# Where the feed-forward's operands begin in on-chip memory: one small tile made 96 bytes longer

## The chip, the cores and the metric

The kernel runs on one core of a Trainium2 chip. TensorE (PE in the profile) multiplies, VectorE (DVE) and ScalarE (ACT) work on elements, SyncE (SP) issues most of the transfers, GpSimd (POOL) a few. A matrix product takes two instructions: one loads the stationary operand of 128 x 128 into the array (PEld in the profile), one streams the moving operand of up to 512 columns past it (PE). Both operands are read from the on-chip memory, in which every tile takes the same bytes on each of 128 partitions; "the place" of a tile is the byte at which it begins on a partition.

The metric is the device time of one execution in microseconds (us); a lower time is better.

## The reference, cut to what matters

One layer of a hybrid backbone for 1024 latent tokens and 256 context tokens of width 1024. Two token mixers (a gated linear attention and a gated delta rule) read the normalised input, their outputs are merged and projected by `w_out`, and a SwiGLU feed-forward and a final norm follow. The part that this change bears on:

```python
x = x + mod_l[2] * y_l                       # y_l = merged @ w_out
x = x + mod_l[5] * swiglu(modulate(rmsnorm(x, norm2_w), mod_l[3], mod_l[4]),
                          ffn_w_gate, ffn_w_up, ffn_w_down)
return rmsnorm(x, final_norm_w)

def swiglu(t, w_gate, w_up, w_down):
    return (jax.nn.silu(t @ w_gate) * (t @ w_up)) @ w_down
```

`x` is 1024 x 1024, `w_gate` and `w_up` are 1024 x 2816, `w_down` is 2816 x 1024, all float32.

## The kernel before, in words

There are three phases, one after the other. Phase 1 normalises the input, projects it and runs the gated linear attention; phase 2 runs the gated delta rule and the gates; phase 3, from about 1575 us on, is the output projection, the second norm and the feed-forward.

A float32 product is made of three products in a rounded format (`mm3`, lines 167 to 173): each operand is split into a high part (rounded by ACT) and a low part (what is left, by DVE), and high x high (L171), high x low (L172) and low x high (L173) add up in one bank of PSUM. So the large products are long rows of one form of matmul: 128 x 128 stationary, 512 columns moving, each with a weight load of its own. In the names of the profile, `ch<-hh,whi` is a matmul into a bank `ch`, with `hh` moving and `whi` stationary. Trailing numbers are left out, so `hh` stands for `hh0` and `hh1`.

In phase 3:

- **Output projection** (L1134 to L1136): stationary is the merged mixer output in `hh`/`hl` (high and low), moving is `w_out`, which lies in `xh`/`xl`. 8 token tiles x 2 halves x 24 matmuls, 384 in all, in banks `pj`.
- **Second norm** (`norm2`, L1145): after each two token tiles, DVE works out the norm's factors, PE turns the tokens with a diagonal matrix (L1161, plain float32), and ACT and DVE write the high and low part back into `hh`/`hl`, which from then on hold the normalised input.
- **Gate and up projection** (L1184 to L1192): for each of 22 tiles of the hidden width, 16 stationary blocks of each weight (`whi`, `wlo`, split from `wraw` at L153 and L154 into a ring of four buffers), the normalised input `hh`/`hl` moving, in two halves of 512 tokens. 22 x 2 x 2 x 24 = 2112 matmuls, in banks `ch` (gate) and `pj` (up).
- **Down projection** (L1207 to L1213): the activations (kept in `xh`) are stationary, the rows of `w_down` (kept in `xl`) move. The 22 tiles come in groups of 2 or 3, and after each group DVE adds the 16 partial results to `x1`. In the last group the final norm and the store of each token tile follow at once.

Where things lie is decided by pools, which stack in the order in which they are opened; a tile takes its bytes rounded up to 32. In phase 3 the order is `xp` (`xh`, `xl`), `x1p`, `wp2` (the weights' `wraw`, `whi`, `wlo`), `f1` (`a2`, `m5`, `fw`, `ms3`, `mh`, `rs3`), `hp` (`hh0`, `hh1`, `hl0`, `hl1`), `f2` (the rest). All tiles of `xp`, `x1p` and `wp2` have lengths that are multiples of 2048 bytes; so have those in front of the weights in phases 1 and 2. `f1` takes 32 + 4096 + 4096 + 32 + 64 + 32 = 8352 bytes, which is 65 x 128 + 32. From the built program, in bytes:

| tiles | begin at | remainder by 128 | remainder by 512 |
|---|---|---|---|
| `xh`, `xl` (all phases) | 18112, 50880 | 64 | 192 |
| `whi`, `wlo` of phase 1, first buffers | 104128, 112320 | 64 | 192 |
| `whi`, `wlo` of phase 3, first buffers | 120512, 128704 | 64 | 192 |
| `hh0`, `hh1`, `hl0`, `hl1` | 145248 + i x 16384 | 96 | 352 |
| `draw`, `a`, `tmp2`, `junk3` in `f2` | from 210784 | 96 | 352 |

The blocks that one matmul or one weight load takes out of these tiles begin at multiples of 512 bytes from the tile's start, so the remainders hold for each of them.

Of the kernel before, what the change touches and what calls it, by code (L numbers as in the profile page):

```python
# [8 lines left out]
F32 = mybir.dt.float32  # L9
# [8 lines left out]
P = 128  # L18
# [57 lines left out]
class Layer:  # L76
# [1095 lines left out]
    def ffn(self, f1, f2, x1, hh, hl):  # L1172
        nc, I = self.nc, self.I
        m5 = f1.tile([P, D], F32, name="m5")
        nc.sync.dma_start(m5, self.mrow[5].broadcast_to([P, D]))
        fw = f1.tile([P, D], F32, name="fw")
        nc.sync.dma_start(fw, I['final_norm_w'].rearrange("(o n) -> o n", o=1).broadcast_to([P, D]))
        groups = [range(a, b) for a, b in zip((0, 2, 4, 7, 10, 13, 16, 19), (2, 4, 7, 10, 13, 16, 19, 22))]
        ms = f1.tile([P, 8], F32, name="ms3")
        mh = f1.tile([P, 8, 2], F32, name="mh")  # L1180
        rs = f1.tile([P, 8], F32, name="rs3")
        for gi, g in enumerate(groups):
            acts, downs = [], []
            for f in g:  # L1184
                wg = self.wcols(I['ffn_w_gate'], f * P)
                wu = self.wcols(I['ffn_w_up'], f * P)
                ah, al = self.xh[:, f % 4, :], self.xh[:, 4 + f % 4, :]
                for n in range(2):
                    ns = slice(n * 512, n * 512 + 512)
                    pg, pu = self.ch(P, 512), self.pj(P, 512)  # L1190
                    for ps, w in ((pg, wg), (pu, wu)):
                        self.mm3(ps, [(w[k][0], w[k][1], hh[n][:, k, :], hl[n][:, k, :]) for k in range(KT)])  # L1192
                    a = f2.tile([P, 512], F32, tag="a", name="a", bufs=4)
                    nc.scalar.activation(a, pg, AF.Tanh, scale=0.5)
                    nc.vector.scalar_tensor_tensor(a, a, 1.0, pg, ALU.add, ALU.mult)
                    nc.vector.tensor_tensor(a, a, pu, ALU.mult)  # L1196
                    nc.scalar.activation(ah[:, ns], a, AF.Copy)  # L1197
                    nc.vector.tensor_tensor(al[:, ns], a, ah[:, ns].bitcast(F32), ALU.subtract)
                acts.append((ah, al))
                raw = f2.tile([P, D], F32, tag="draw", name="draw")  # L1200
                nc.sync.dma_start(raw, I['ffn_w_down'][f * P:(f + 1) * P, :])
                nc.vector.tensor_tensor(raw, raw, m5, ALU.mult)
                dh, dl = self.xl[:, f % 4, :], self.xl[:, 4 + f % 4, :]
                nc.scalar.activation(dh, raw, AF.Copy)  # L1204
                nc.vector.tensor_tensor(dl, raw, dh.bitcast(F32), ALU.subtract)
                downs.append((dh, dl))
            for t in range(8):  # L1207
                ts = slice(t * P, t * P + P)
                for n in range(2):
                    ns = slice(n * 512, n * 512 + 512)  # L1210
                    ps = (self.pj if gi == len(groups) - 1 and n else self.wk)(P, 512)
                    self.mm3(ps, [(a[0][:, ts], a[1][:, ts], w[0][:, ns], w[1][:, ns]) for a, w in zip(acts, downs)])
                    nc.vector.tensor_tensor(x1[:, t, ns], x1[:, t, ns], ps, ALU.add)  # L1213
                    if gi == len(groups) - 1:
                        junk = f2.tile([P, 512], F32, tag="a", name="junk3", bufs=4)
                        nc.scalar.activation(junk, x1[:, t, ns], AF.Square, accum_out=mh[:, t, n:n + 1])
                if gi == len(groups) - 1:
                    m, r = ms[:, t:t + 1], rs[:, t:t + 1]
                    nc.vector.tensor_tensor(m, mh[:, t, 0:1], mh[:, t, 1:2], ALU.add)
                    nc.vector.tensor_scalar(m, m, 1.0 / D, EPS, ALU.mult, ALU.add)  # L1220
                    self.rsqrt(f2, r, m, 1, "fr")
                    nc.vector.scalar_tensor_tensor(x1[:, t, :], x1[:, t, :], r, fw, ALU.mult, ALU.mult)  # L1222
                    nc.sync.dma_start(self.out[ts, :], x1[:, t, :])
# [35 lines left out]
```

## Time and profile before

| | |
|---|---|
| median of 3 runs | 2439.49 us (2432.53 to 2444.21) |
| profiled execution | 2438.06 us, of which its span is 2436.3 us |
| PE busy in the span | 2346.7 us (96%) |
| DVE, ACT busy | 65%, 45% |
| mean granted TensorE clock | 0.987 of full speed |

How to read it: the share of busy time of PE hides how fast it works, since consecutive matmuls overlap in the records (a record of 0.39 us is followed by the next one 0.23 us later). What a stretch of matmuls costs is read from the starts of its first and last matmul and their number. An engine's row ends with the idle time before its instructions and with what released them; idle time of an engine that PE does not wait for costs nothing.

### The profile page before, as it was taken

The page shows a single profiled execution, that of the slowest core. Times are in us where ns is not written, and L with a number is a line of the kernel's source. Part 1 is how long each engine was busy: PE and PEld are TensorE (multiplying, and loading weights), DVE is VectorE, ACT ScalarE, POOL GpSimd, SP SyncE. Part 2 cuts the span into 40 slices and gives each one's busy share as a digit, 9 for nine tenths or more (in the row PEclk, how much of TensorE's full clock was granted, in tenths as well). Part 3 has the DMA queues.
Part 4 walks back from the last instruction along what each step waited for, and adds up shares of the span by engine and source line. Part 5 has one row for each costly group of instructions (what it writes and reads, how often), then busy time and mean ns, then how long its engine had stood idle before and what let it go on. Part 6 is the DMA issues. An engine that isn't in the chain of part 4 may idle for free. (4 is left out here: it accounts for less than half of the span.)

```text
span 2436.3 us, 37019 instructions
## 1 busy us (share of the span) xinstructions
PE 2346.7 (96%) x13868; PEld 1932.4 (79%) x13868; DVE 1583.7 (65%) x3855; ACT 1100.0 (45%) x2691; POOL 68.7 (3%) x138
## 2 busy tenths in 40 slices
PE   7999999999999889999999999899999999999998
PEld 5978988988988668777777877677888888888886
DVE  6479589489499577888888876655543434334336
ACT  7265165265265556876886676433112112121112
POOL 0000000000000000000000000000000000000000
PEclk9999999999999999999999999899999999999999
DMA  8212412313312532333333233241211111111101
GB/s 286 67 29 71 141 27 89 120 27 102 115 27 90 168 104 76 112 88 103 92 94 115 76 93 100 78 147 36 60 36 55 52 39 57 40 56 48 35 27 69
DMA packets 199106, 197.77 MB, mean 81 GB/s; under 512 B 13715, under 2 KB 166619, under 8 KB 198927
## 3 DMA queue, kind: packets, MB, share of 16 engines
q1 hardware_dynamic: 186096, 159.12, 21.9%
q0 software_dynamic: 10016, 35.19, 4.1%
q8 instruction: 109, 1.79, 0.3%
q10 hardware_dynamic: 2815, 1.11, 0.2%
q14 instruction: 70, 0.57, 0.1%
HBM read 164.13 MB, written 31.23 MB: 80 GB/s over the span
## 5 line engine op out<-in xcount | busy, mean ns | idle before, releaser
L171 PE MATMUL pj<-xh,whi 128*128 128x512 f32 x1040 | 426.1, 410 | 4.9 <-ACT cout L785 3.2
L173 PE MATMUL pj<-xh,wlo 128*128 128x512 f32 x1040 | 424.0, 409 | 2.8 <-DVE wlo L154 2.8
L172 PE MATMUL pj<-xl,whi 128*128 128x512 f32 x1040 | 424.7, 408 | 0.2 <-DVE xl L333 0.2
L153 ACT ACTIVATE whi<-wraw 128x512 fp32r<-128x512 f32 x232 | 145.8, 630 | 304.7 <-PE pj L172 109.9
L154 DVE TENSOR_TENSOR wlo<-wraw,whi 128x512 fp32r<-128x512 f32 x232 | 159.0, 690 | 120.3 <-ACT whi L153 119.4
L171 PEld LDWEIGHTS pj<-xh,whi 128*128 128x128 f32 x1040 | 198.0, 190 | 38.1 <-ACT cout L785 3.8
L173 PEld LDWEIGHTS pj<-xh,wlo 128*128 128x128 f32 x1040 | 197.4, 190 | 35.6 <-DVE wlo L154 3.1
L172 PEld LDWEIGHTS pj<-xl,whi 128*128 128x128 f32 x1040 | 197.9, 190 | 31.9 <-DVE xl L333 0.5
L1213 DVE TENSOR_TENSOR x<-x,wk 128x512 f32<-128x512 f32 x120 | 82.5, 687 | 113.7 <-PE wk L173 113.4
L171 PE MATMUL ch<-hh,whi 128*128 128x512 f32 x352 | 139.6, 397 | 0.0
L172 PE MATMUL ch<-hl,whi 128*128 128x512 f32 x352 | 139.6, 397 | 0.0
L171 PE MATMUL pj<-hh,whi 128*128 128x512 f32 x352 | 139.6, 397 | 0.0
L172 PE MATMUL pj<-hl,whi 128*128 128x512 f32 x352 | 139.6, 397 | 0.0
L173 PE MATMUL pj<-hh,wlo 128*128 128x512 f32 x352 | 139.6, 397 | 0.0
L173 PE MATMUL ch<-hh,wlo 128*128 128x512 f32 x352 | 139.6, 396 | 0.0
L171 PE MATMUL wk<-xl,xh 128*128 128x512 f32 x328 | 127.7, 389 | 0.0
L172 PE MATMUL wk<-xl,xh 128*128 128x512 f32 x328 | 127.7, 389 | 0.0
L173 PE MATMUL wk<-xl,xh 128*128 128x512 f32 x328 | 127.6, 389 | 0.0
L793 DVE SCALAR_TENSOR_TENSOR cout<-cin,cw,cout 128x896 f32<-128x896 f32 (+1 forms) x96 | 113.4, 1181 | 3.7 <-ACT cout L785 3.7
L1204 ACT ACTIVATE xl<-draw 128x1024 fp32r<-128x1024 f32 x22 | 22.5, 1054 | 196.6 <-PE wk L173 189.2
L1196 DVE TENSOR_TENSOR a<-a,pj 128x512 f32<-128x512 f32 x44 | 30.3, 688 | 114.4 <-PE pj L173 114.4
L1197 ACT ACTIVATE xh<-a 128x512 fp32r<-128x512 f32 x44 | 27.8, 632 | 128.4 <-DVE a L1196 128.4
(392 smaller groups left out, 5458.9 us busy)
## 6 DMA issues: line engine op xcount, KB each, us to landing
wraw<-in_w_in_dram SPq DMA_DIRECT2D x144, 256.0 KB, 3.0
mw<-in_w_mod_dram SPq DMA_DIRECT2D x64, 256.0 KB, 4.0
wraw<-in_ffn_w_gate_dram SPq DMA_DIRECT2D x44, 256.0 KB, 2.9
draw<-in_ffn_w_down_dram SPq DMA_DIRECT2D x22, 512.0 KB, 4.0
wraw<-in_ffn_w_up_dram SPq DMA_DIRECT2D x44, 256.0 KB, 2.9
bc<-rows SPq DMA_DIRECT2D x80, 128.0 KB, 3.1
wm<-in_w_mod_dram SPq DMA_DIRECT2D x16, 512.0 KB, 3.7
A<-rows SPq DMA_DIRECT2D x64, 128.0 KB, 3.2
```

Source lines behind the costliest of these rows:

```text
L153: nc.scalar.activation(hi, raw, AF.Copy)
L154: nc.vector.tensor_tensor(lo, raw, hi.bitcast(F32), ALU.subtract)
L171: self.nc.tensor.matmul(ps, ah, bh, start=(first and i == 0), stop=False)
L172: self.nc.tensor.matmul(ps, ah, bl, start=False, stop=False)
L173: self.nc.tensor.matmul(ps, al, bh, start=False, stop=(last and i == n - 1))
L793: nc.vector.scalar_tensor_tensor(o, cl[:, :, lo + s:16 + hi + s], tap(i), o, ALU.mult, ALU.add)
L1196: nc.vector.tensor_tensor(a, a, pu, ALU.mult)
L1197: nc.scalar.activation(ah[:, ns], a, AF.Copy)
L1204: nc.scalar.activation(dh, raw, AF.Copy)
L1213: nc.vector.tensor_tensor(x1[:, t, ns], x1[:, t, ns], ps, ALU.add)
```

## The change

The tile `ms3`, which holds one number per token tile for the final norm, gets 32 columns of float32 where it had 8. The code still uses columns 0 to 7. The same instructions stand in the same order on every engine, with the same shapes.

```diff
         groups = [range(a, b) for a, b in zip((0, 2, 4, 7, 10, 13, 16, 19), (2, 4, 7, 10, 13, 16, 19, 22))]
-        ms = f1.tile([P, 8], F32, name="ms3")
+
+        ms = f1.tile([P, 32], F32, name="ms3")
         mh = f1.tile([P, 8, 2], F32, name="mh")
         rs = f1.tile([P, 8], F32, name="rs3")
```

`f1` then takes 8448 bytes = 66 x 128, and what is allocated behind `ms3` moves up by 96 bytes: `mh` and `rs3`, then `hh` and `hl`, then all of `f2`. `hh0` begins at 145344, with a remainder of 64 by 128 and of 448 by 512; the tiles `draw`, `a`, `tmp2` and `junk3` of `f2` get the remainder 64 by 128 too. `xh`, `xl`, `x1` and the weights stay where they are.

## Rows read from the trace of the kernel before

**Rows 1.** The page: the span, PE's busy time, and the granted clock in 40 slices of the span.

```profile
span 2436.3 us, 37019 instructions
...
PE 2346.7 (96%) x13868; PEld 1932.4 (79%) x13868; DVE 1583.7 (65%) x3855; ACT 1100.0 (45%) x2691; POOL 68.7 (3%) x138
...
PEclk9999999999999999999999999899999999999999
```

**Rows 2.** The view of waits for PE alone, from 1686 us to the end: all that it lists (us in total, times, longest).

```profile
PE wk L1161 <- issue: 1.0, 1, 1.0
```

**Rows 3.** The page's groups by line: two of the six groups of the gate and up projection (each x352) and one of the three of the down projection; busy us, mean ns of one record, idle before.

```profile
L171 PE MATMUL ch<-hh,whi 128*128 128x512 f32 x352 | 139.6, 397 | 0.0
...
L173 PE MATMUL pj<-hh,wlo 128*128 128x512 f32 x352 | 139.6, 397 | 0.0
...
L171 PE MATMUL wk<-xl,xh 128*128 128x512 f32 x328 | 127.7, 389 | 0.0
```

**Rows 4.** The timeline of PE from 1935 to 1975 us, inside the gate and up projection of one group of tiles: start us, length us, line, operands. First two and last of 172 consecutive matmuls.

```profile
1934.78 0.40 PE L172 MATMUL pj<-hl,whi 128*128 128x512 f32 x1
1935.01 0.40 PE L173 MATMUL pj<-hh,wlo 128*128 128x512 f32 x1
...
1974.84 0.40 PE L172 MATMUL pj<-hl,whi 128*128 128x512 f32 x1
```

**Rows 5.** The same view from 1897 to 1912 us, inside a down projection: first and last of 68 consecutive matmuls.

```profile
1896.81 0.39 PE L171 MATMUL wk<-xl,xh 128*128 128x512 f32 x1
...
1911.99 0.39 PE L172 MATMUL wk<-xl,xh 128*128 128x512 f32 x1
```

**Rows 6.** The same view from 1643 to 1664 us, inside the output projection: three of a stretch that repeats itself, and the ends of 90 consecutive matmuls.

```profile
1642.83 0.40 PE L171 MATMUL pj<-xh,hh 128*128 128x512 f32 x1
...
1645.41 0.39 PE L173 MATMUL pj<-xh,hl 128*128 128x512 f32 x1
1645.64 0.40 PE L171 MATMUL pj<-xh,hh 128*128 128x512 f32 x1
1645.88 0.39 PE L172 MATMUL pj<-xl,hh 128*128 128x512 f32 x1
...
1663.61 0.40 PE L173 MATMUL pj<-xh,hl 128*128 128x512 f32 x1
```

**Rows 7.** The same view in phase 1, 740.5 to 744 us: a projection that follows other matmuls. Between the first and the second row shown lie 8 matmuls, between the second and the third 3.

```profile
740.86 0.40 PE L173 MATMUL pj<-xh,wlo 128*128 128x512 f32 x1
...
742.94 0.39 PE L173 MATMUL pj<-xh,wlo 128*128 128x512 f32 x1
...
743.85 0.39 PE L171 MATMUL pj<-xh,whi 128*128 128x512 f32 x1
```

**Rows 8.** Busy time in three stretches of 10 us: two in down projections and one in a gate and up projection. Columns: stretch, its us, then busy us and (instructions) of PE, PEld, DVE, ACT, POOL, then granted clock, DMA share, GB/s.

```profile
1802.00:1812.00 10.00, 10.00 (x46) 8.28 (x45) 6.18 (x10) 1.26 (x2) 0.00 (x0) 1.00 0.17 49
1900.00:1910.00 10.00, 10.00 (x46) 8.29 (x45) 3.24 (x6) 0.00 (x0) 0.00 (x0) 1.00 0.01 2
1760.00:1770.00 10.00, 10.00 (x44) 8.05 (x43) 4.07 (x6) 1.23 (x2) 0.00 (x0) 1.00 0.35 105
```

**Rows 9.** Groups by line: the output projection's first products over the whole run, and all its matmuls from 1578 to 1592 us.

```profile
L171 PE MATMUL pj<-xh,hh 128*128 128x512 f32 x128 | 52.9, 415 | 4.3 <-ACT hh L1122 3.4 <-DVE d L1138 0.9
...
L171 PE MATMUL pj<-xh,hh 128*128 128x512 f32 x15 | 7.4, 502 | 3.4 <-ACT hh L1122 3.4
L172 PE MATMUL pj<-xl,hh 128*128 128x512 f32 x14 | 6.3, 464 | 0.0
L173 PE MATMUL pj<-xh,hl 128*128 128x512 f32 x13 | 5.9, 457 | 0.0
```

**Rows 10.** The timeline around the last second norm: PE's turn of the tokens.

```profile
1695.82 2.02 PE L1161 MATMUL wk<-diag,x 128*128 128x128 f32 x16 [0.98 <-issue]
```

**Rows 11.** The view of waits from 1735 to 2395 us: what the weights' split and the rows of `w_down` waited for.

```profile
ACT whi L153 <- PE pj L172: 75.8, 39, 2.2
...
DVE draw L1202 <- DMA draw<-in_ffn_w_down_dram: 14.6, 11, 2.6
```

**Rows 12.** Groups by line of ACT and DVE with the same work on tiles of either remainder: `wraw`, `whi`, `wlo` have 64, `a` has 96.

```profile
L154 DVE TENSOR_TENSOR wlo<-wraw,whi 128x512 fp32r<-128x512 f32 x232 | 159.0, 690 | 120.3 <-ACT whi L153 119.4
...
L1198 DVE TENSOR_TENSOR xh<-a,xh 128x512 fp32r<-128x512 f32 x44 | 30.4, 692 | 17.2 <-ACT xh L1197 15.4
L1197 ACT ACTIVATE xh<-a 128x512 fp32r<-128x512 f32 x44 | 27.8, 632 | 128.4 <-DVE a L1196 128.4
```

**Rows 13.** The end: PE's last matmul in the timeline, and the last step of the chain that ended last.

```profile
2424.41 0.39 PE L173 MATMUL pj<-xl,xh 128*128 128x512 f32 x1
...
2431.21 1.28 DVE x L1222
```

## The prediction

> **What bounds the kernel now.** I read the page first: PE is busy for 2346.7 of 2436.3 us, at the full clock in nearly every slice [rows 1]. Then the waits for PE in phase 3: from 1686 us to the end it waits once, for 1.0 us [rows 2]. So the feed-forward takes as long as its matmuls take, and no transfer, split or bank holds it up. What remains is how fast one matmul follows another. The groups by line hint at a difference: the same form of matmul has records of 397 ns in the gate and up projection and of 389 ns in the down projection [rows 3]. Records overlap, so I took the timeline and divided the time between two starts by the number of steps:
>
> - gate and up, 171 steps: (1974.84 - 1934.78) / 171 = 234.3 ns [rows 4];
> - down, 67 steps: (1911.99 - 1896.81) / 67 = 226.6 ns [rows 5];
> - output projection, 89 steps: (1663.61 - 1642.83) / 89 = 233.5 ns [rows 6].
>
> The form, the clock and the number of weight loads are the same in all three. The neighbours' work doesn't sort them: the down stretch at 1802 us has 6.18 us of DVE and 1.26 us of ACT in 10 us, the one at 1900 us has 3.24 and nothing, and both start 46 matmuls; the gate and up stretch at 1760 us, with DVE between the two (4.07), has 44 [rows 8]. The bank doesn't either: phase 1 projects into `pj`, as the output projection does, and gets to the fast step there: after other work, 9 steps in (742.94 - 740.86) us or 231 ns each, then 4 in (743.85 - 742.94) us or 227.5 ns, which is 226.6 within the rounding of the rows [rows 7].
>
> What does sort them is where the two operands lie. Down (`xl` moving, `xh` stationary) and phase 1 (`xh` and the weights) have both operands at remainder 64 by 128 bytes: 226.6 ns. Gate and up (`hh` 96, weights 64) and the output projection (`xh` 64, `hh` 96) have them 32 bytes apart: 234.3 and 233.5 ns. The output projection is the telling one, since there `hh` is stationary and the other operand moves. My reading: while one matmul streams, the next one's weights are read from the same memory; with equal remainders the two reads fall into a step that hinders them least after a few matmuls, with unequal ones they never do.
>
> **The change part by part.**
>
> *Gate and up.* `hh` and `hl` get the weights' remainder, so I let these matmuls go at the down projection's step: 6 groups of 352 are 2112 matmuls [rows 3], 2112 x (234.3 - 226.6) ns = 16.3 us. Nothing of it lies beside other work, since PE waits for nothing there. The two ends: if each of them stayed in what phase 1 shows ahead of the fast step, 231 ns [rows 7], it would be 2112 x 3.3 = 7.0 us; by the records' means, 397 against 389 [rows 3], 2112 x 8 = 16.9 us. I take 16.3, nearest to the down projection, which has the same long unbroken rows of matmuls.
>
> *Output projection.* It gets equal remainders too. Of its 384 matmuls (three products of 128) 15 + 14 + 13 = 42 lie before 1592 us, where they are stretched by the arrival of their inputs, with records of 457 to 502 ns [rows 9]; I give them nothing. The others: 342 x (233.5 - 226.6) ns = 2.4 us. After each turn of tokens in the second norm (L1161) the step has to be found again, for 9 matmuls at 231 instead of 226.6 ns, 0.04 us each time; with some eight such breaks that is 0.3 us, which leaves 2.1 us. Ends: 0 and 2.4 us.
>
> *What is late next.* The last second norm is a chain over DVE, ACT and PE, and PE already waits 0.98 us in it [rows 10]. The 9 us of gate and up that PE does meanwhile shrink by 3.3%, 0.3 us, while the chain keeps its length, so I take 0.3 us off; at worst the output projection's 2.1 us go there as well. In the rest of the feed-forward the weights' split waits for PE to give a buffer back (75.8 us in total for the group shown), not the other way round [rows 11]. A gate buffer is needed again 36 matmuls after its last use (12 of gate, 24 of up), 8.2 us at the new step, and the split needs 0.63 us on ACT and 0.69 on DVE [rows 12]: covered. The rows of `w_down` are waited for by DVE alone, 14.6 us in 11 waits, while PE waits for none [rows 2, 11].
>
> *The rest.* `draw`, `a`, `tmp2` and `junk3` also change their remainder from 96 to 64. For ACT and DVE that is worth nothing: DVE's subtraction takes 690 ns on tiles at 64 and 692 with `a` at 96 [rows 12]. The end, from PE's last matmul at 2424.41 us to DVE's last product at 2431.21 and the store [rows 13], is DVE's and stays as it is. The longer tile itself is never read or written beyond column 7: 0.
>
> Sum: 16.3 + 2.1 - 0.3 = 18.1 us, less 0.1 for three breaks in the first gate and up products: 18.0 us. Against the profiled execution, 2438.1 (its span and 1.8 us around it), that is 2420.1 us. The median of the runs shown is 1.4 us above that execution, so I predict 2421.5 us for the median, 0.74% less.
>
> **A rule that speaks against it.** The rows say that matmuls with a weight load beside each differ by 7.7 ns with nothing else different but places [rows 4, 5]. The Trainium skill says otherwise ("TensorE: Matmul & The Clock Gate", Part 2, step on LDWEIGHTS): PE has two independent read ports, and "Loading the next tile's weights doesn't steal SBUF read bandwidth from the running matmul." By that rule places could not matter and the sum would be 0. The trace doesn't tell which port waits, but a difference that follows the places in four kinds of stretch is hard to square with it.
>
> **The rivals.**
>
> *No change* (the rule's result, as a mechanism of this kernel). `hh` and `hl` have something else in common: they are the only operands of these products above 136896 bytes, behind the weights' ring, and are used in phase 3 alone. If that makes the 7 ns, the shift leaves it: 2439.5 us. For it: every slow stretch has `hh` or `hl` as an operand, so the trace can't part place and tile. Against it: it has no reason why phase 1's products begin at 231 ns and then drop to 227 [rows 7], which looks like two reads falling into step.
>
> *The distance that counts isn't 128 bytes.* All fast pairs are equal even by 512 bytes (192 and 192). After the change `hh` has 448 and the weights 192: equal by 128 and 256, 256 bytes apart by 512. If the reads repeat over 512 bytes, the new distance is one that the trace doesn't show. It would then lie between 231 ns, the better steps of the slow stretches and phase 1's beginning, and the old 234.3: from 2439.5 - 2112 x 3.3 ns = 2432.5 to 2439.5 us, say 2436.
>
> *Slower.* The same mechanism with the other sign: at 256 bytes apart by 512 the reads meet more often than at 160. The output projection's pattern contains steps of 0.24 us (1645.64 to 1645.88) beside shorter ones [rows 6]; if all gate and up matmuls had that, 2112 x (240 - 234.3) ns = 12.0 us, and 342 x 6.5 ns = 2.2 us more for the output projection: 2453.7 us. It is slower by more than 0.5% from a step of about 239 ns on.
>
> **How the numbers follow.** I tell changes apart from 0.5%, about 12 us here. The forecast has 0.77, no change 0.10, the other distance 0.08, slower 0.05. The forecast's own range is 2415 to 2431: 7.0 us for gate and up with 1.8 for the output projection at the weak end (2430.7), 16.9 + 2.4 at the strong end (2420.2), and some 5 us for the scatter of runs, which reached from 2432.5 to 2444.2 before. The whole range, 2414 to 2434, takes in the better half of the other distance and leaves out no change and slower. Faster by over 0.5% (under 2427.3): 0.77 of the forecast but for its weak end, 0.76 in all; slower by over 0.5%: 0.04; within: 0.20.
>
> **What would show it.** In the timeline of gate and up, 171 steps should take 38.7 us instead of 40.1, with single steps of 226 to 227 ns and none of 238; the records of `ch<-hh,whi` should have a mean of 389 ns; the output projection should step at 227 ns within some ten matmuls of each break; the down projection should stay at 226.6. PE's waits after 1686 us should still add up to under 2 us. I am wrong if gate and up still step at 231 ns or more, or if a wait for a split or for `w_down` appears in PE's rows.

## The result and the profile after

The changed kernel takes 2425.03 us in the median of 7 runs (2421.66 to 2438.4), the kernel before 2441.66 us (2432.53 to 2444.21) beside it. The ratio is 0.9942 with a 95% interval of 0.9917 to 0.9967, about 14 us less (the two medians lie 16.6 us apart). The last experiment measured it once more: 2420.25 against 2439.52 us, ratio 0.9922 (0.9889 to 0.9956).

The profiled execution of the changed kernel hides this at first. Its page has nearly the same span as before (2436.3 us), and next to it the records that were to become shorter:

```profile
span 2436.6 us, 37019 instructions
...
PEclk9999999999999986999999999989999999999999
...
L171 PE MATMUL ch<-hh,whi 128*128 128x512 f32 x352 | 137.0, 389 | 0.0
...
L171 PE MATMUL wk<-xl,xh 128*128 128x512 f32 x328 | 127.6, 389 | 0.0
```

Gate and up now have the down projection's mean of 389 ns, where they had 397 [rows 3]. What ate the gain in this one execution is the dip of the clock in the 15th and 16th slice: a stretch of phase 2, work that the change doesn't touch, ran at half clock. The view of stretches shows it for the changed kernel (us, busy us and instructions of PE, PEld, DVE, ACT, POOL, granted clock, DMA share, GB/s):

```profile
898.00:953.00 55.00, 53.97 (x366) 40.69 (x367) 11.85 (x31) 25.57 (x65) 2.28 (x5) 0.50 0.18 56
```

The same view of the kernel before, where that place went at full clock and PE began 436 matmuls in 45 us instead of 366 in 55:

```profile
905.00:950.00 45.00, 44.57 (x436) 34.70 (x427) 24.42 (x79) 33.34 (x109) 2.28 (x5) 1.00 0.27 80
```

So phase 3 has to be looked at by itself. Its first matmul started at 1578.10 us before:

```profile
1578.10 0.79 PE L171 MATMUL pj<-xh,hh 128*128 128x512 f32 x1 [2.68 <-ACT hh L1122]
```

The timeline of the changed kernel, with its first and last matmul of phase 3, the output projection after a break, and gate and up:

```profile
1596.06 0.79 PE L171 MATMUL pj<-xh,hh 128*128 128x512 f32 x1 [2.66 <-ACT hh L1122]
...
1658.95 0.39 PE L171 MATMUL pj<-xh,hh 128*128 128x512 f32 x1
...
1661.02 0.39 PE L171 MATMUL pj<-xh,hh 128*128 128x512 f32 x1
...
1678.92 0.39 PE L172 MATMUL pj<-xl,hh 128*128 128x512 f32 x1
...
1941.76 0.39 PE L172 MATMUL pj<-hl,whi 128*128 128x512 f32 x1
...
1976.90 0.39 PE L171 MATMUL pj<-hh,whi 128*128 128x512 f32 x1
...
2424.79 0.39 PE L173 MATMUL pj<-xl,xh 128*128 128x512 f32 x1
```

From the first to the last matmul phase 3 took 2424.41 - 1578.10 = 846.3 us before [rows 13] and takes 2424.79 - 1596.06 = 828.7 us now: 17.6 us less. A step is the time from the start of one matmul to the start of the next. In gate and up 155 steps take 35.14 us, 226.7 ns each, against 234.3 [rows 4]. The output projection steps at 230 ns for 9 matmuls after a break (1658.95 to 1661.02) and at 226.6 ns for the 79 that follow (to 1678.92), against 233.5 [rows 6]. The view of waits for PE from 1690 us on lists one, 1.3 us where it was 1.0 [rows 2]:

```profile
PE wk L1161 <- issue: 1.3, 1, 1.3
```

### The profile page after: what moved, and what is told of

Its sections match the earlier page's. It is cut to its first block, busy times and chain, and to the rows that moved or that the text cites. A ratio compares the mean times of both kernels' runs of the same rounds, so it can differ in the third digit from the quotient of the medians.

```text
span 2436.6 us, 37019 instructions
## 1 busy us (share of the span) xinstructions
PE 2345.5 (96%) x13868; PEld 1943.6 (80%) x13868; DVE 1583.5 (65%) x3855; ACT 1099.5 (45%) x2691; POOL 68.7 (3%) x138
## 5 line engine op out<-in xcount | busy, mean ns | idle before, releaser
L173 PE MATMUL pj<-xh,wlo 128*128 128x512 f32 x1040 | 427.2, 412 | 2.8 <-DVE wlo L154 2.8
L172 PE MATMUL pj<-xl,whi 128*128 128x512 f32 x1040 | 427.8, 411 | 0.2 <-DVE xl L333 0.2
L173 PEld LDWEIGHTS pj<-xh,wlo 128*128 128x128 f32 x1040 | 199.0, 191 | 35.9 <-DVE wlo L154 3.1
L172 PEld LDWEIGHTS pj<-xl,whi 128*128 128x128 f32 x1040 | 199.2, 192 | 32.2 <-DVE xl L333 0.5
L172 PE MATMUL ch<-hl,whi 128*128 128x512 f32 x352 | 137.1, 389 | 0.0
L172 PE MATMUL pj<-hl,whi 128*128 128x512 f32 x352 | 137.0, 389 | 0.0
L173 PE MATMUL pj<-hh,wlo 128*128 128x512 f32 x352 | 137.0, 389 | 0.0
L173 PE MATMUL ch<-hh,wlo 128*128 128x512 f32 x352 | 136.9, 389 | 0.0
L172 PE MATMUL wk<-xl,xh 128*128 128x512 f32 x328 | 127.6, 389 | 0.0
L173 PE MATMUL wk<-xl,xh 128*128 128x512 f32 x328 | 127.6, 389 | 0.0
```

The lines of the kernel that those rows point to most:

```text
L172: self.nc.tensor.matmul(ps, ah, bl, start=False, stop=False)
L173: self.nc.tensor.matmul(ps, al, bh, start=False, stop=(last and i == n - 1))
```

## The experiments

The question left by the result: what is it about the place? The prediction's answer was equal remainders by 128 bytes. The load beside a matmul is the weight load for the next matmul, and the distance of the two is where the moving operand begins minus where that load begins, of which the remainder by 256 (or by 128) is given. By 256 bytes, gate and up had a distance of 160 before and have 0 now; by 128 bytes, 32 and 0. The first four experiments change the length of the small tile or shift the weights as well; every edit is made in the changed kernel. In each fence below, the first two rows are the ends of a stretch of the output projection and the last two the ends of a stretch of gate and up, unless said otherwise; the steps are worked out from them and the number of matmuls, both ends counted, so there is one step fewer. Each step comes from one profiled execution, from a stretch at the full granted clock (1.00). Experiments 1 to 4 and 7 to 11 were executed once, so their whole times are not compared.

**1. Half of 128 bytes apart.**

```diff
-        ms = f1.tile([P, 32], F32, name="ms3")
+        ms = f1.tile([P, 16], F32, name="ms3")
```

> The small tile 16 columns long: hh and hl begin at remainder 0 by 128, 64 bytes from the weights. Theory of places by 128 bytes: gate and up step at 230 to 238 ns, the output projection at 230 to 238 ns, the down projection at 226.6 ns. Rival, the reads repeat over 64 bytes: both step at 226.6 ns, as in the changed kernel. Rival, only the old place was bad: 226.6 ns too.

```profile
1642.67 0.39 PE L171 MATMUL pj<-xh,hh 128*128 128x512 f32 x1
...
1659.84 0.39 PE L171 MATMUL pj<-xh,hh 128*128 128x512 f32 x1
...
1941.69 0.39 PE L172 MATMUL pj<-hl,whi 128*128 128x512 f32 x1
...
1976.93 0.39 PE L173 MATMUL ch<-hh,wlo 128*128 128x512 f32 x1
```

With 76 and 152 matmuls that is 228.9 ns in the output projection and 233.4 ns in gate and up. Neither is the 226.6 ns of the two rivals, so neither 64 bytes nor "anything but the old place" is the rule. But 228.9 ns is also below the 230 to 238 ns expected, and that the two stages differ was not expected either, since 64 bytes by 128 is the same in both directions. The down projection, whose operands did not move, steps at 226.7 ns (131 matmuls from 1890.07 to 1919.54 us).

**2. The old distance with the other sign.** The tile has 24 columns (`[P, 24]`).

> The small tile 24 columns long: hh and hl begin at remainder 32 by 128, 96 bytes from the weights (the old distance with the other sign). Theory of places by 128 bytes: gate and up step at 230 to 238 ns in a pattern of their own, the output projection (whose distance has the sign of gate and up before) in the pattern that gate and up had before, 234 ns. Rival, only the old place was bad: 226.6 ns in both.

```profile
1642.66 0.39 PE L171 MATMUL pj<-xh,hh 128*128 128x512 f32 x1
...
1659.93 0.39 PE L173 MATMUL pj<-xh,hl 128*128 128x512 f32 x1
...
1941.73 0.40 PE L172 MATMUL pj<-hl,whi 128*128 128x512 f32 x1
...
1976.96 0.40 PE L173 MATMUL ch<-hh,wlo 128*128 128x512 f32 x1
```

75 and 152 matmuls: 233.4 and 233.3 ns. Slow in both, as expected; but the output projection has not taken over the 234 ns of gate and up before, a first sign against 128.

**3. Equal by 128, not by 256.** The tile has 64 columns (`[P, 64]`).

> The small tile 64 columns long: hh and hl begin at remainder 64 by 128, but 128 bytes from the weights by 256 and 384 by 512, where the changed kernel has 0 and 256. Theory of places by 128 bytes: gate and up and the output projection step at 226.6 to 227 ns as in the changed kernel. Rival, the reads repeat over 256 bytes: 230 to 238 ns.

```profile
1642.68 0.39 PE L173 MATMUL pj<-xh,hl 128*128 128x512 f32 x1
...
1659.87 0.40 PE L172 MATMUL pj<-xl,hh 128*128 128x512 f32 x1
...
1941.84 0.39 PE L173 MATMUL pj<-hh,wlo 128*128 128x512 f32 x1
...
1976.84 0.39 PE L173 MATMUL ch<-hh,wlo 128*128 128x512 f32 x1
```

75 and 151 matmuls: 232.3 and 233.3 ns. The theory of 128 bytes falls: all operands have the same remainder by 128 here, and of the 7.6 ns gained in gate and up 1.0 is left.

**4. All at another remainder.** A tile of 32 bytes in the pool ahead of the weights puts weights, `hh` and `hl` at 96 by 128, with `xh` and `xl` left at 64.

```diff
             x1 = x1_pool.tile([P, T // P, D], F32, name="x1")
+            x1_pool.tile([P, 8], F32, name="gap")
```

> The changed kernel with a tile of 32 bytes ahead of the weights of phase 3: weights, hh and hl all at remainder 96 by 128, xh and xl still at 64. Theory of the distance between the two operands: gate and up step at 226.6 ns (both at 96), the output projection (xh 64, hh 96) at 233.5 ns, the down projection at 226.6. Rival, remainder 64 is a good place in itself: gate and up at 230 ns or more.

```profile
1660.65 0.40 PE L171 MATMUL pj<-xh,hh 128*128 128x512 f32 x1
...
1677.92 0.40 PE L173 MATMUL pj<-xh,hl 128*128 128x512 f32 x1
...
1941.79 0.39 PE L171 MATMUL pj<-hh,whi 128*128 128x512 f32 x1
...
1976.92 0.39 PE L173 MATMUL pj<-hh,wlo 128*128 128x512 f32 x1
```

75 and 156 matmuls: the output projection at 233.4 ns, gate and up at 226.6, as the theory of the distance has it. No place is good by itself.

**5. Equal by 512 too, timed.** The tile has 96 columns (`[P, 96]`), which gives all operands the remainder 192 by 512; the changed kernel has 256 between `hh` and the weights.

> The small tile 96 columns long: hh and hl begin at remainder 192 by 512, as the weights, xh and xl do. New theory (the reads repeat over 256 bytes, since 128 bytes apart was slow and 256 was fast): the same as the changed kernel, 226.6 to 227 ns in gate and up and in the output projection, phase 3 about 17.6 us shorter than before, ratio 0.990 to 0.997. Rival, the reads repeat over 512 bytes with a second good place at 256: the step is below 226 ns or the output projection finds it faster, and phase 3 is shorter by over 18 us.

```profile
1941.62 0.39 PE L173 MATMUL ch<-hh,wlo 128*128 128x512 f32 x1
...
1976.97 0.39 PE L173 MATMUL pj<-hh,wlo 128*128 128x512 f32 x1
```

Gate and up step at 226.6 ns (157 matmuls, the ends of which are shown), the output projection at 226.7. The ratio is 0.9929 (0.9902 to 0.9955), and phase 3 lasts from 1575.53 to 2405.37 us, 829.8 us. So 0 and 256 by 512 are the same to the reads, and the distance counts by 256.

**6. The third kernel, timed.**

> The kernel of the third experiment (remainder by 128 equal, 128 bytes apart by 256), timed. Theory of 256 bytes: phase 3 is 1 to 2 us shorter than before, the ratio 0.997 to 1.001, so that equal remainders by 128 alone are worth nothing that can be told. Theory of 128 bytes, if the one profile was an exception: 0.990 to 0.997.

Ratio 0.9988 (0.9964 to 1.0013), in the same series as the fifth. Equal remainders by 128 alone bring nothing that can be told in the time. In the profile phase 3 is 843.6 us long (1575.84 to 2419.40), 2.7 us less than before, where 1 to 2 were expected: gate and up step at 233.3 ns here too.

**7. One pair in three.** `hl` alone is moved 32 bytes on.

```diff
-            hh, hl = ([hp.tile([P, KT, 512], F32R, name=f"{n}{i}") for i in range(2)] for n in ("hh", "hl"))
+            hh = [hp.tile([P, KT, 512], F32R, name=f"hh{i}") for i in range(2)]
+            hp.tile([P, 8], F32, name="gap")
+            hl = [hp.tile([P, KT, 512], F32R, name=f"hl{i}") for i in range(2)]
```

> The changed kernel with a tile of 32 bytes between hh and hl: hh 0 by 256 from the weights, hl 32. In gate and up one matmul in three streams hl, while wlo is loaded. Theory, the moving operand and the load beside it must agree, matmul by matmul: two thirds of the steps at 226 to 227 ns, one third at 230 or more, mean 229 ns. Rival, one pair in three upsets the step of all: no step at 226 to 227 in long rows, mean 231 to 234 ns. In the output projection hl is a load: the same two answers, there with the slow step at the matmul beside which hl is loaded (xl moving) or, if a matmul's own stationary operand counts, at the one with hl stationary.

Gate and up step at 231.6 ns (153 matmuls from 1941.69 to 1976.90 us), the output projection at 233.4 ns. One unequal pair in three upsets the others, as the rival said: no step is back at 226.6 ns. Which pair pays shows in the output projection, from 1644 to 1661 us, in the timeline and in the records by line (busy us, mean ns of one):

```profile
1644.44 0.40 PE L172 MATMUL pj<-xl,hh 128*128 128x512 f32 x1
1644.68 0.39 PE L173 MATMUL pj<-xh,hl 128*128 128x512 f32 x1
1644.91 0.40 PE L171 MATMUL pj<-xh,hh 128*128 128x512 f32 x1
1645.14 0.40 PE L172 MATMUL pj<-xl,hh 128*128 128x512 f32 x1
...
L172 PE MATMUL pj<-xl,hh 128*128 128x512 f32 x25 | 10.0, 400 | 0.0
L173 PE MATMUL pj<-xh,hl 128*128 128x512 f32 x25 | 9.7, 389 | 0.0
L171 PE MATMUL pj<-xh,hh 128*128 128x512 f32 x24 | 9.5, 395 | 0.0
```

From L172, beside which `hl` is being loaded for L173, to the next start it is 240 ns each time, and 230 after the other two. The records say the same: L172 has the longest, 400 ns, and the matmul that has `hl` as its own stationary operand (L173) the shortest, 389. So it is the running matmul and the load beside it that meet, not a matmul and its own weights.

**8. The distance 64 with the other sign.** The tile has 48 columns (`[P, 48]`): gate and up get 64 by 256, where they had 192 in the first experiment.

> The small tile 48 columns long: hh and hl 64 bytes from the weights by 256 (192 in the first experiment). Theory of 256 bytes: gate and up at 228 to 236 ns, not at 226.6; if the sign of the distance matters as the first experiment's output projection suggests (64 by 256 seen from the moving operand, 229.2 ns), gate and up step near 229 ns here. Theory without a sign: 233.3 ns, as in the first experiment.

```profile
1941.66 0.39 PE L173 MATMUL ch<-hh,wlo 128*128 128x512 f32 x1
...
1976.91 0.39 PE L171 MATMUL ch<-hh,whi 128*128 128x512 f32 x1
```

Gate and up step at 228.9 ns (155 matmuls, the ends of which are shown), the output projection at 233.3. That is the first experiment with its stages exchanged: the sign counts.

**9 and 10. The rest of the circle.** Tiles of 40 and of 56 columns (`[P, 40]`, `[P, 56]`), with the step forecast from the other stage's value at the same distance.

> The small tile 40 columns long: hh and hl have the old remainder of 96 by 128, but are 32 bytes from the weights by 256, where they were 160. Theory, the step is a function of (moving operand minus the load beside it) by 256 bytes, whatever the tiles: gate and up step at 233.4 ns, which the output projection had at this distance in the second experiment; the output projection is at 224 by 256 and steps at 233.3 ns, which gate and up had there. Rival, a function of 128 bytes: gate and up step at 234.3 ns in the old pattern (231, 234, 235, 237, 238).

> The small tile 56 columns long: hh and hl 96 bytes from the weights by 256, the output projection at 160. Theory of 256 bytes with a sign: gate and up step at 233.6 ns, the output projection's value before, and the output projection at 234.3 ns, gate and up's value before: the two stages change places. Rival, each stage has its own value: gate and up 234.3, the output projection 233.5.

In the ninth, gate and up step at 233.3 ns (151 matmuls from 1941.80 to 1976.80 us) and the output projection at 233.4: the forecasts were 233.4 and 233.3, and the old remainder by 128 doesn't bring the old 234.3 back. The tenth:

```profile
1659.79 0.39 PE L172 MATMUL pj<-xl,hh 128*128 128x512 f32 x1
...
1676.90 0.40 PE L173 MATMUL pj<-xh,hl 128*128 128x512 f32 x1
...
1941.83 0.39 PE L172 MATMUL ch<-hl,whi 128*128 128x512 f32 x1
...
1976.83 0.39 PE L172 MATMUL pj<-hl,whi 128*128 128x512 f32 x1
```

74 and 151 matmuls: the output projection at 234.4 ns, gate and up at 233.3. They have changed places, within 0.3 ns.

**11. The down projection and phase 1 made slow.** A tile of 32 bytes between `xh` and `xl` moves `xl`, the weights, `hh` and `hl` on together and leaves `xh`; to make room, the scratch tile `th` of the first steps is dropped and its values are worked out in `sc`.

```diff
             self.xh = xp.tile([P, KT, T], F32R, name="xh")
+            xp.tile([P, 8], F32, name="gap")
             self.xl = xp.tile([P, KT, T], F32R, name="xl")
...
-            th = vp.tile([P, 16], F32, name="th")
+            self.sc = c.tile([P, 16], F32, name="sc")
+            th = self.sc
             nc.scalar.activation(th, self.vec[:, 64:80], AF.Tanh, scale=0.5)
-            self.sc = c.tile([P, 16], F32, name="sc")
```

> The changed kernel with a tile of 32 bytes between xh and xl (and one scratch tile of the first steps merged with its result, to make room): xl, the weights, hh and hl move on together, xh stays. The down projection, untouched so far, now has xl moving 32 bytes from the loads of xh. Theory of places: it steps at 233.4 ns, 1056 x 6.7 = 7 us longer, gate and up keep 226.7, the output projection, in which two of three matmuls move xh beside a load of hh, 230 to 233 ns; phase 3 is 8 to 10 us longer than in the changed kernel; phase 1's long rows, with the same two of three, step at 230 to 233 ns instead of 226.6. Rival, the effect hangs on the tiles hh and hl: the down projection stays at 226.7.

The timeline (lines are one higher here): the ends of a stretch of 45 matmuls in phase 1, of 126 in a down projection, and of 156 in gate and up.

```profile
261.65 0.39 PE L173 MATMUL pj<-xl,whi 128*128 128x512 f32 x1
...
271.91 0.40 PE L172 MATMUL pj<-xh,whi 128*128 128x512 f32 x1
...
1889.83 0.39 PE L172 MATMUL wk<-xl,xh 128*128 128x512 f32 x1
...
1919.00 0.40 PE L174 MATMUL wk<-xl,xh 128*128 128x512 f32 x1
...
1941.70 0.39 PE L172 MATMUL pj<-hh,whi 128*128 128x512 f32 x1
...
1976.84 0.39 PE L174 MATMUL ch<-hh,wlo 128*128 128x512 f32 x1
```

The down projection steps at 233.4 ns and phase 1 at 233.2, where the kernel before has 226.6 [rows 5] and, over the same stretch of phase 1, 226.4; gate and up keep 226.7. Phase 1 and the output projection (233.3 ns, 74 matmuls from 1644.96 to 1661.99 us) come out just above the 230 to 233 expected. Phase 3 lasts from 1577.09 to 2414.80 us, 837.7 us, which is 9.0 us more than in the first profile of the changed kernel and 7.7 more than in the second (below), where 8 to 10 were expected. With this the effect is neither one of `hh` and `hl` nor of high addresses: it was made in two stages where neither takes part, and gate and up, whose operands moved on together, stayed fast.

**12. The changed kernel again.**

> The changed kernel once more, timed, and profiled anew. Theory, its profiled execution was long by a stretch at half clock in phase 2 (55 us at 898 us) that kernels of either kind have now and then: phase 3 is again 828 to 830 us long, the span is 2416 to 2421 us if the profile has no such stretch, ratio 0.990 to 0.996. Rival, the stretch comes with the change: it is there again, and the span is about 2436 us.

2420.25 us against 2439.52, ratio 0.9922 (0.9889 to 0.9956). The new profile has a span of 2415.0 us, 1 us below the range expected, and phase 3 lasts 2403.18 - 1573.22 = 830.0 us:

```profile
1573.22 0.80 PE L171 MATMUL pj<-xh,hh 128*128 128x512 f32 x1 [2.61 <-ACT hh L1122]
...
2403.18 0.39 PE L173 MATMUL pj<-xl,xh 128*128 128x512 f32 x1
```

Phase 2 goes at full clock in the stretch that was at half (the same view as above):

```profile
901.00:953.00 52.00, 51.54 (x458) 40.64 (x457) 32.09 (x111) 35.54 (x117) 2.28 (x5) 1.00 0.26 78
```

So the half clock of the first profile does not belong to the change. It is seen with either length of step: of the fourteen profiles, those of experiments 4, 8 and 10 have a granted clock of 0.50 from 902 to 930 us as well, and the other ten don't.

**All distances together.** The step of long rows of 512-column matmuls in one stretch each, by the distance of the moving operand from the load beside it (GU gate and up, OP output projection, DN down projection; the number is the experiment):

| bytes by 256 | ns from start to start |
|---|---|
| 0 | 226.7 (GU changed), 226.6 (OP changed), 226.6 (GU 4), 226.6 (GU 5), 226.7 (OP 5), 226.7 (GU 11), 226.6 (DN before) |
| 32 | 233.3 (GU 9), 233.4 (OP 2), 233.4 (DN 11) |
| 64 | 228.9 (GU 8), 228.9 (OP 1) |
| 96 | 233.3 (GU 10), 233.5 (OP before) |
| 128 | 233.3 (GU 3), 232.3 (OP 3) |
| 160 | 234.3 (GU before), 234.4 (OP 10) |
| 192 | 233.4 (GU 1), 233.3 (OP 8) |
| 224 | 233.3 (GU 2), 233.4 (OP 4), 233.4 (OP 9) |

At 128 bytes stretches of one execution differ by 1 ns: the output projection of the sixth experiment, which has the kernel of the third, steps at 233.4 ns from 1613.82 to 1634.36 us (89 matmuls) and at 232.4 from 1639.47 to 1660.85 (93).

## Why the prediction was right, and where it wasn't

**The bound.** Right: phase 3 is as long as its matmuls take, and 7.6 ns less per step became 17.6 us less in phase 3, where 18.0 were forecast. The second profile has 846.3 - 830.0 = 16.3 us, the fifth experiment's 16.5.

**Gate and up, 16.3 us.** The step went to 226.7 ns, so 2112 x (234.3 - 226.7) ns = 16.0 us. From the first matmul of gate and up to the last of the kernel it was 738.9 us before (1685.54 to 2424.41) and is 723.3 or 723.4 in the first and second profile and the fifth experiment's: 15.5 or 15.6 us less, with the longer wait below in it. The choice of the down projection's step, rather than phase 1's beginning at 231 ns, was right.

**Output projection, 2.1 us.** Its step fell to 226.6 ns nine matmuls after a break, as the term had it. The time hit the term in one profile only. From its first matmul to the first of gate and up it was 107.4 us before (1578.10 to 1685.54); it is 105.4 in the first profile of the changed kernel (to 1701.42), but 106.6 in the second (to 1679.85) and in the fifth experiment's (1575.53 to 1682.10). That is 2.1 us less, then 0.8 to 0.9. The view of waits for PE, from the first of these matmuls to 1720 us, adds up to 5.6 us before and to 6.7, 7.7 and 7.5 now, so 1.1 to 2.1 us of what the faster matmuls gave went to waits. The second profile has one at the first turn of tokens that isn't listed before:

```profile
PE wk L1161 <- DVE diag L1155: 1.3, 1, 1.3
```

So it was in part luck that the first profile gave 2.1 us. The sum had such a wait for the last second norm alone, with the whole term going there "at worst". Why it is 0.3 us in the first profile and 1.3 in the two others isn't shown.

**What is late next, 0.3 us.** The wait in the last second norm grew from 1.0 to 1.3 us, as forecast. No wait for a split or for `w_down` appeared among PE's.

**The reading of the place.** Here a step failed, though not the sum: "with equal remainders [by 128 bytes] the two reads fall into a step that hinders them least". The trace of before could not tell 128 from 256, since all its fast pairs were equal by both. The third and the sixth experiment did: equal by 128 and 128 apart by 256 is slow (233.3 ns) and worth nothing that can be told in the time (0.9988, 0.9964 to 1.0013). The forecast came true because the change of 96 bytes closes the distance by 256 as well; as far as the rule goes, that was luck. The rival of another period was right that 128 isn't the number, and wrong about 512, under which the changed kernel would have been 256 bytes off.

**The rival of no change.** Its mechanism, that `hh` and `hl` are slow for another reason than their place, is refuted by the result, where the same tiles still lie above 136896 bytes and step at 226.7 ns, and by the eleventh experiment. By the rule beside it, loading the next weights takes no read bandwidth from the running matmul (the Trainium skill, "TensorE: Matmul & The Clock Gate", Part 2, step on LDWEIGHTS). The runs don't agree in so far as the two are not independent in time: the same 512 columns step at 226.6 to 234.4 ns, by where the load beside them reads. Which of the two waits isn't shown. The records of the weight loads in gate and up have 188 to 189 ns before and 187 to 188 in the changed kernel, those of the matmuls 397 and 389; that points to the matmul, but the ends of matmul records are modelled by the profile. That the step is least at equal places by 256 bytes is what was measured, and a picture of banks behind it would only be argued.

**The slower rival.** No distance tried was slower than the old one by more than 0.1 ns, so its price was never within reach.

**The time.** 2421.5 us was forecast, 2425.03 and in the larger series 2420.25 us came out. Between the two profiles of the changed kernel, whose spans differ by 21.6 us, the difference lies ahead of phase 3 (its first matmul starts at 1596.06 and at 1573.22 us) and not in the steps of gate and up, which differ by under 0.1 ns. Where the executions without a profile differ isn't shown.

## What to carry to other kernels

When long rows of one form of matmul differ by a few per cent between stages, divide the time between two starts by the number of steps, and compare where the moving operand and the next stationary operand lie: here they had to be a multiple of 256 bytes apart, and every other distance tried (in steps of 32 bytes) cost 1 to 3.4%. A pad costs a few bytes of on-chip memory, for which the eleventh experiment had to make room. It has to be checked for all pairs that run side by side, since one unequal pair in three slowed the others too (230 ns beside 240). A trace in which two explanations fall together (128 and 256 bytes) can carry the forecast and still not the rule; one cheap run with the pad that parts them is worth having before the rule is written down.

## What the runs showed that was not expected

- The distance has a sign. At 64 bytes by 256 the step is 228.9 ns, at 192 it is 233.3 to 233.4, in two stages with exchanged roles. At 96 and 160 it differs by 1 ns, at 32 and 224 it doesn't.
- Equal places don't work at once: after a break the step is 230 to 231 ns for 9 matmuls [rows 7] and 226.6 to 227.5 from then on, in phase 1 as in the output projection.
- The clock. PE waited 3.4 us for ACT ahead of the stretch that went at half clock in the first profile of the changed kernel (from 894 to 898 us PE was busy for 1.61 of 4 us). The profile of the fifth experiment has the same wait of 3.4 us at the same place, and there the granted clock is back at 1.00 from 906 us on, while it stayed at 0.50 to 953 us here, with PE busy for 53.97 of 55 us at the lower of its two levels, 1.2 GHz. It cost this execution as much as the change gains, some 18 us (phase 3 began at 1596.06 instead of 1578.10 us). What decides between the two was not tried.
